# Expert numbers from bf16 step sums, lo parts kept on one engine, and a one-hot from fourfold copies: one change to a fused two-block kernel

## The chip, the cores and the metric

The kernel runs on one core of a Trainium2 chip. The metric is the device time of one execution in microseconds, as the median of several runs. The engines are named as in the profile: PE (TensorE, matmuls), PEld (its weight loads), DVE (VectorE), ACT (ScalarE), POOL (GpSimd) and SP (SyncE, which issues the DMAs).

## The reference, cut to what matters

Two blocks are applied to x of 256 tokens by 1024 features, in float32. The first is a retention and sparse-attention mixer with a gated convolution FFN. The second is a mixer of a gated linear recurrence (HGRN) and a long convolution (Hyena), and then PEER, a layer of 128 x 128 = 16384 experts. The change is in the second block, mostly in PEER:

```python
qh = (xb @ w_q).reshape(T, 8, 2, 128)
s = einsum('thpc,hpnc->thpn', qh, sk)              # scores against 2 x 128 sub-keys
s1, i1 = top_k(s[:, :, 0], 16)
s2, i2 = top_k(s[:, :, 1], 16)
cand_s = (s1[..., :, None] + s2[..., None, :]).reshape(T, 8, 256)
cand_i = (i1[..., :, None] * 128 + i2[..., None, :]).reshape(T, 8, 256)
top_s, pos = top_k(cand_s, 16)
experts = take_along_axis(cand_i, pos, axis=-1)
g = softmax(top_s)
act = gelu(einsum('td,thkd->thk', xb, u[experts])) * g
out = einsum('thk,thkd->td', act, v[experts])
```

## The kernel before, in words

**Products of float32 by two parts.** A weight tile of 128 x 1024 floats comes in by one DMA (`chunk`, tile `wraw`, four buffers). ACT writes its high part `whi` (three buffers) and then DVE or POOL writes the rest, `wlo = wraw - whi` (three buffers). A product takes three matmuls: whi with the high and the low part of the activations, then wlo with the high part. `lin_a` issues, for one chunk, 16 matmuls that read whi and then 8 that read wlo. `chunk` has an argument `pool_lo`, the share of its calls whose wlo goes to POOL.

**PEER as a dense layer.** The kernel does not gather experts. For each of the 128 values of i1 there is a chunk of u (`u_blocks`: one chunk, 24 matmuls into one PSUM tile `ax`, then ACT's gelu into the tile `gs`), and later a chunk of v (`v_blocks`). The activations are multiplied in between by a matrix of gate weights, which `weigh` makes for 8 tokens at a time: `prep` compares the key numbers with a row of numbers (the one-hot `o1` for the first key, `o2` for the second, and three bf16 parts of g in `gT` times o2), 24 small matmuls turn them into 4 x 128 x 128 weights in two `ax` tiles, and DVE (for blocks that are done) or ACT (for those that are not) puts them into `gs`. The first 48 u blocks come before `weigh` starts, the other 80 run beside it. A u block whose tokens are partly weighed keeps its gelu in a tile `gl`, and DVE multiplies it into `gs`.

**The top 16.** Sixteen chunks of w_q give the key scores; DVE finds 16 of 128 for each half (`first_tops`). The generator `topk` does the rest, 128 tokens (one half) at a time: 50 candidate sums in `cs`, the 16 best with their places `px`, then the expert numbers. For these the kernel before builds the same 50 candidates of the numbers (`ce`), compares each place with 0 to 49 (`eq`, 3200 elements for four heads), multiplies by `ce` (`em`), and adds up over the candidates (`ei`). The result is split into two key numbers by shifts of integers (`ii`, `fi`).

**The order.** The code pushes generators aside (`beside`) and takes steps from them between chunks (`pump`). In the kernel before, `pump` holds a step back while a count of DVE's work stands ahead of a count of PE's; the class `Counted` wraps both engines to keep those counts. The framework's scheduler then fixes each engine's order; every engine runs its own list in order and waits on semaphores. Through the wrapper, almost all instructions of PE and DVE carry line L220.

The four PSUM tiles `ax` are shared by u blocks, weights and transposes; the output accumulates in the other four.

Of the kernel before, what the change touches and what calls it, by code (L numbers as in the profile page):

```python
# [189 lines left out]
def tile_block(ctx: ExitStack, tc: tile.TileContext, a, out):  # L190
# [17 lines left out]

    clock = {"pe": 0.0, "dve": 0.0}

    class Counted:
        def __init__(self, engine, cost):
            self.engine, self.cost = engine, cost

        def __getattr__(self, name):
            f = getattr(self.engine, name)

            def call(*args, **kw):
                self.cost(name, args)
                return f(*args, **kw)  # L220

            return call

    def elements(ap):
        return math.prod(ap.shape[1:])

    def tensor_cost(name, args):
        n = elements(args[2])
        if name == "transpose":
            c = 0.11  # L230
        elif args[1].dtype == F32:
            c = 4 * n / 2400 + 0.005
        else:
            c = n / 2400 + (0.0135 if args[1].dtype == F32R else 0.0025)
        clock["pe"] += c

    def vector_cost(name, args):
        n = elements(args[1]) if name in ("tensor_reduce", "max") else \
            elements(args[2]) if name == "max_index" else elements(args[0])
        if args[0].dtype == BF:  # L240
            n //= 2
        clock["dve"] = max(clock["dve"], clock["pe"] - 3.0) + (n + 150) / 960

    PE, DVE = Counted(nc.tensor, tensor_cost), Counted(nc.vector, vector_cost)

    ident = cons.tile([128, 128], F32, name="ident")
    mhalf = cons.tile([128, 8], F32, name="mhalf")
    DVE.memset(mhalf, -0.5)
# [6 lines left out]
    def step():  # L255
        side = sides[0]
        try:
            next(side[0])
            side[1] = clock["dve"]
        except StopIteration:  # L260
            sides.pop(0)

    def pump(n, wait=True):


        while n > 0 and sides and (not wait or sides[0][1] <= clock["pe"]):
            step()
            n -= 1

    def beside(gen):  # L270
        sides.append([gen, 0.0])
        return gen

# [19 lines left out]
    def chunk(src, n=1024, pool_lo=0.0, gate=None):  # L293

        r = wp.tile([128, n], F32, name="wraw", bufs=NRAW)
        nc.sync.dma_start(r, src)
        hi = wp.tile([128, n], F32R, name="whi", bufs=NHI)
        if gate is not None:
            DVE.tensor_copy(hi[:, 0:1], gate[0][:, 0:1])
        nc.scalar.activation(hi, r, AF.Copy)  # L300
        lo = wp.tile([128, n], F32R, name="wlo", bufs=3)
        if gate is not None:
            DVE.tensor_copy(lo[:, 0:1], gate[1][:, 0:1])
        cnt[0] += 1
        eng = nc.gpsimd if (cnt[0] * pool_lo) % 1.0 + pool_lo >= 1.0 else DVE
        eng.tensor_tensor(lo, r, f32(hi), OP.subtract)  # L306
        return hi, lo

    def split(hi, lo, src):
        nc.scalar.activation(hi, src, AF.Copy)  # L310
        DVE.tensor_tensor(lo, src, f32(hi), OP.subtract)

    def lin_a(ps, w, xs, pool=None):

        (wh, wl), (xh, xl) = w, xs
        for k in range(8):
            s = slice(k * 128, k * 128 + 128)
            PE.matmul(ps, wh[:, s], xh[:, k, :], start=(k == 0), stop=False)
            PE.matmul(ps, wh[:, s], xl[:, k, :], start=False, stop=False)
        for k in range(8):  # L320
            s = slice(k * 128, k * 128 + 128)
            PE.matmul(ps, wl[:, s], xh[:, k, :], start=False, stop=(k == 7))

    def lin_b(ps2, w, xs, k0, nk, first, last, n=512, tiles=(0, 1)):

        (wh, wl), (xh, xl) = w, xs
        for i in tiles:
            ti = slice(i * 128, i * 128 + 128)
            for q, (wt, xt) in enumerate(((wh, xh), (wh, xl), (wl, xh))):
                for k in range(nk):  # L330
                    PE.matmul(ps2[i], xt[:, k0 + k, ti], wt[:, k * n:(k + 1) * n],
# [9 lines left out]
    def rstd_of(ss, n, scale, eps):  # L341
        DVE.tensor_scalar(ss, ss, scale, eps, op0=OP.mult, op1=OP.add)
# [6 lines left out]
    def rstd_sum(ss):  # L349
        DVE.tensor_tensor(ss[:, 0:1], ss[:, 0:1], ss[:, 1:2], OP.add)  # L350
# [8 lines left out]
    class Norm:  # L359
# [13 lines left out]
        def weigh(self, i):  # L373
            self.xw[i] = act.tile([128, D], F32, name="xn", bufs=2)
            for h in range(2):
                DVE.tensor_tensor(self.xw[i][:, half(h)], self.x[:, i, half(h)], self.nw[:, half(h)], OP.mult)

        def ready(self, i):
            r = rstd_sum(self.ss[i])
            self.dg[i] = act.tile([128, 128], F32, name="diag", bufs=2)  # L380
            DVE.tensor_scalar(self.dg[i], ident, r, None, op0=OP.mult)

        def turn(self, i):
            ti = slice(i * 128, i * 128 + 128)
# [8 lines left out]
    class Post:  # L393
# [6 lines left out]
        def piece(self, i, h, ps):  # L400
# [4 lines left out]
            DVE.tensor_tensor(self.y[i][:, half(h)], ps, self.nw[:, half(h)], OP.mult)  # L405

        def finish(self, i):
            r = rstd_sum(self.ss[i])
            for h in range(2):
                xh = self.x[:, i, half(h)]  # L410
                DVE.scalar_tensor_tensor(xh, self.y[i][:, half(h)], r, xh, op0=OP.mult, op1=OP.add)
# [10 lines left out]
    def filters(fp):  # L422
# [15 lines left out]
        for l, wt in enumerate((fw1, fw2)):  # L438
            p = pax([128, T])
            PE.matmul(p[:64], wt, hid, start=True, stop=True)  # L440
            y = fp.tile([64, T], F32, name="siny")
            DVE.tensor_scalar(y, p[:64], fvec[:, 2 * l:2 * l + 1], fvec[:, 2 * l + 1:2 * l + 2],
                                    op0=OP.add, op1=OP.mult)
            n = fp.tile([64, T], F32, name="sinn", bufs=1)
            DVE.tensor_scalar(n, y, float(np.float32(1 / (2 * math.pi))), 12582912.0, op0=OP.mult, op1=OP.add)
            DVE.tensor_scalar(n, n, -12582912.0, None, op0=OP.add)
# [10 lines left out]
        for j in range(8):  # L457
# [41 lines left out]
    for _ in range(16):  # L499
        PE.matmul(wps, warm[:, :128], warm, start=True, stop=True)  # L500
# [81 lines left out]
    def tables():  # L582
# [7 lines left out]
        DVE.tensor_copy(identb, ident)  # L590
        DVE.tensor_copy(cmask, nsac[:, 0:128])
# [14 lines left out]
    def rope_rest(dst, q, n, cos, sin):  # L606
        p2 = pax([128, T])
        PE.matmul(p2[:, :n], perm, q[:, :n], start=True, stop=True)
# [3 lines left out]
        DVE.tensor_tensor(t2[:, :n], p2[:, :n], sin, OP.mult)  # L612
        DVE.tensor_tensor(dst, t1[:, :n], t2[:, :n], OP.add)

    def proj_v():
        pv = [[pmm([128, 512]) for _ in range(2)] for _ in range(2)]
        for k in range(8):
            wh, wl = pre[k] if k < 2 else chunk(a["wb1"][k], 792)
            for i in range(2):
                ti = slice(i * 128, i * 128 + 128)  # L620
                for q, (wt, xt) in enumerate(((wh, hT[0]), (wh, hT[1]), (wl, hT[0]))):
                    st, en = (k == 0 and q == 0), (k == 7 and q == 2)
                    PE.matmul(pv[i][0], xt[:, k, ti], wt[:, 0:512], start=st, stop=en)
                    PE.matmul(pv[i][1][:, :280], xt[:, k, ti], wt[:, 512:792], start=st, stop=en)
            if k > 2:
                pump(1)
        for i in range(2):
            nc.scalar.activation(gate[:, i, :], pv[i][1][:, 256:280], AF.Sigmoid)
            DVE.tensor_copy(vb[:, i, 0:512], pv[i][0])
            DVE.tensor_copy(vb[:, i, 512:768], pv[i][1][:, 0:256])  # L630

    def proj(j, bank=pmm):
# [6 lines left out]
        elif j < 12:  # L639
            fl, pos = flat["kv"[j - 10]]  # L640
            v = ps.rearrange("p (n a b) -> p a n b", a=8, b=2)
            for g in range(2):
                gs_ = slice(g * 64, g * 64 + 64)
                for par in range(2):
                    for half in range(2):
                        hs = slice(half * 8, half * 8 + 8)
                        DVE.tensor_tensor(
                            fl[par * 64:par * 64 + 64, hs, g, 0:15], v[gs_, :, half:half + 15, par],
                            pos[gs_, par, hs].unsqueeze(2).to_broadcast([64, 8, 15]), OP.add)
        else:  # L650
            h = j - 12
            nc.scalar.activation(decay[:, h, :], ps, AF.Copy)
            DVE.tensor_scalar(silT[:, h, :], ps, gnw[:, h:h + 1], None, op0=OP.mult)

    def compress():

        hidT, w2 = {}, {}
        for s in "kv":
            fl, pos = flat[s]
            ph = pax([128, 256])  # L660
            for c in range(4):
                w1 = wp.tile([128, 4, 256], F32, name="wraw", bufs=NRAW)
# [10 lines left out]
            for c in range(2):  # L673
                PE.matmul(pt[:, c, :], part[:, c * 128:c * 128 + 128], stack, start=True, stop=True)
# [907 lines left out]
```

## Time and profile before

| | us |
|---|---|
| median of 3 runs | 1624.26 (1622.09 to 1625.32) |
| the profiled execution's own time | 1621.0 |
| its span, first to last instruction | 1619.2 |
| PE busy in the span | 1561.6 (96%) |
| DVE busy | 1166.7 (72%) |
| ACT busy | 799.8 (49%) |
| POOL busy | 368.3 (23%) |

The stages by time from the span's start: first block to 391; second block's mixer from there to 757; w_q chunks to about 816; 128 u blocks to 1263, of which the first 48 end at 985; v blocks to the end. PE's matmuls overlap, so the spacing of starts is read, not the length of one.

### The profile page before, as it was taken

Reading aid. Unit: us, or ns where it says so; the run is one execution under the profiler, and the core shown is the slowest. Engines: PE = TensorE matmul, PEld = TensorE weight load, DVE = VectorE, ACT = ScalarE, POOL = GpSimd, SP = SyncE. Lnnn points to the kernel's source line nnn. Section 1 sums busy time; section 2 is a strip of 40 time slices with the busy share of each in tenths; the row PEclk is TensorE's granted clock in tenths of the full one; section 3 lists DMA queues with packets and bytes.
Section 4 is the critical chain, followed back from the end, with each engine's and each line's share of the span. In section 5 each row is a group of like instructions: output and inputs, shape, how many; then the busy total and the mean of one; then the engine's idle time right before and its main releaser. Section 6 shows DMA issues by size and latency. Waiting matters only on the chain.

```text
span 1619.2 us, 30408 instructions
## 1 busy us (share of the span) xinstructions
PE 1561.6 (96%) x12014; PEld 1401.1 (87%) x12014; DVE 1166.7 (72%) x2041; ACT 799.8 (49%) x1383; POOL 368.3 (23%) x204
## 2 busy tenths in 40 slices
PE   8999999999999989999987899999999999999998
PEld 7775899978987977987987899999999888888886
DVE  6585787846688696775799915999999655555554
ACT  4454565545744634544543344544434455555444
POOL 0122333112112112102767861111123000000000
PEclk9999999999999999999989999999999999999999
DMA  7731555554653443554433455444444655555553
GB/s 255 253 103 37 178 181 182 193 174 159 203 183 119 158 141 108 166 179 169 160 124 119 150 190 183 146 155 147 155 144 142 210 195 193 194 190 192 194 193 117
DMA packets 78646, 268.59 MB, mean 166 GB/s; under 512 B 9991, under 2 KB 12328, under 8 KB 78376
## 3 DMA queue, kind: packets, MB, share of 16 engines
q1 hardware_dynamic: 78216, 266.13, 49.6%
q8 instruction: 94, 1.54, 0.4%
q10 hardware_dynamic: 288, 0.52, 0.1%
q14 instruction: 48, 0.39, 0.1%
HBM read 263.47 MB, written 3.15 MB: 165 GB/s over the span
## 4 chain that ended last, share of the span: by engine, by line
PE 66%; DVE 8%; issue 1%; ACT 0%; POOL 0%; POOLq 0%; DVEq 0%; ACTq 0%
PE mm L220 39%; PE ax L220 27%; DVE ei L220 1%; DVE em L220 1%; DVE eq L220 1%; DVE cs L220 1%; DVE o L220 0%; DVE ii L220 0%; DVE px L220 0%; DVE sx L220 0%; DVE hk L220 0%; DVE wlo L220 0%; DVE QA L220 0%; DVE xf L220 0%; DVE ce L220 0%
## 5 line engine op out<-in xcount | busy, mean ns | idle before, releaser
L300 ACT ACTIVATE whi<-wraw 128x1024 fp32r<-128x1024 f32 (+1 forms) x474 | 500.2, 1056 | 514.8 <-PE mm L220 340.0
L220 DVE TENSOR_TENSOR wlo<-wraw,whi 128x1024 fp32r<-128x1024 f32 (+1 forms) x365 | 444.8, 1220 | 322.1 <-ACT whi L300 316.8
L306 POOL TENSOR_TENSOR wlo<-wraw,whi 128x1024 fp32r<-128x1024 f32 x109 | 294.0, 2707 | 593.1 <-ACT whi L300 500.9
L220 PE MATMUL ax<-hThi,whi 128*128 128x256 f32 x1184 | 299.8, 290 | 12.5 <-ACT whi L300 11.7
L220 PE MATMUL ax<-hTlo,whi 128*128 128x256 f32 x1184 | 295.0, 286 | 0.2 <-DVE hTlo L220 0.2
L220 PE MATMUL mm<-whi,aa 128*128 128x512 f32 x1024 | 254.0, 389 | 0.0
L220 PEld LDWEIGHTS ax<-hThi,whi 128*128 128x128 f32 x1184 | 230.5, 195 | 13.6 <-ACT whi L300 12.1
L220 PEld LDWEIGHTS ax<-hTlo,whi 128*128 128x128 f32 x1184 | 230.9, 195 | 0.4 <-DVE hTlo L220 0.4
L220 PEld LDWEIGHTS mm<-whi,aa 128*128 128x128 f32 x1024 | 192.1, 188 | 40.1 <-ACT aa L310 0.3
L220 PE MATMUL mm<-hThi,whi 128*128 128x256 f32 x832 | 207.3, 287 | 1.5 <-ACT whi L300 1.5
L220 PE MATMUL mm<-hTlo,whi 128*128 128x256 f32 x832 | 205.2, 284 | 1.0 <-DVE hTlo L220 1.0
L220 PE MATMUL ax<-hThi,wlo 128*128 128x256 f32 x1184 | 167.8, 285 | 5.1 <-POOL wlo L306 5.1
L220 PEld LDWEIGHTS mm<-hThi,whi 128*128 128x128 f32 x832 | 159.9, 193 | 3.1 <-ACT whi L300 1.9
L220 PEld LDWEIGHTS mm<-hTlo,whi 128*128 128x128 f32 x832 | 160.3, 193 | 1.6 <-DVE hTlo L220 1.5
L220 PEld LDWEIGHTS ax<-hThi,wlo 128*128 128x128 f32 x1184 | 154.0, 193 | 6.2 <-POOL wlo L306 6.2
L220 PE MATMUL mm<-wlo,aa 128*128 128x512 f32 x512 | 137.8, 389 | 0.0
L220 PE MATMUL mm<-hThi,wlo 128*128 128x256 f32 x832 | 117.0, 283 | 0.0
L220 PEld LDWEIGHTS mm<-wlo,aa 128*128 128x128 f32 x512 | 96.1, 188 | 19.9
L220 PEld LDWEIGHTS mm<-hThi,wlo 128*128 128x128 f32 x832 | 107.4, 192 | 0.0
L220 DVE TENSOR_TENSOR o<-o,gTt 128x1024 bf16<-128x1024 bf16 x96 | 92.5, 977 | 1.1
L344 POOL TENSOR_TENSOR rstd<-ssf,mhalf 128x1 f32<-128x1 f32 x2 | 1.1, 544 | 363.1 <-DVE ssf L220 363.1
L1500 ACT ACTIVATE gs<-ax 128x300 f32<-128x300 f32 (+31 forms) x64 | 18.8, 296 | 104.4 <-DVE gs L220 93.6
(347 smaller groups left out, 2128.9 us busy)
## 6 DMA issues: line engine op xcount, KB each, us to landing
wraw<-in_pu_dram SPq DMA_DIRECT2D x128, 512.0 KB, 3.3
wraw<-in_pv_dram SPq DMA_DIRECT2D x128, 512.0 KB, 3.3
wraw<-in_wa_dram SPq DMA_DIRECT2D x64, 512.0 KB, 3.5
wraw<-in_wup_dram SPq DMA_DIRECT2D x44, 512.0 KB, 3.4
wraw<-in_wb_dram SPq DMA_DIRECT2D x32, 512.0 KB, 3.3
wraw<-in_wdn_dram SPq DMA_DIRECT2D x22, 512.0 KB, 3.3
wraw<-in_wq_dram SPq DMA_DIRECT2D x16, 512.0 KB, 3.3
wraw<-in_wo_dram SPq DMA_DIRECT2D x8, 512.0 KB, 3.3
```

What stands on the lines that cost most here:

```text
L220: return f(*args, **kw)
L300: nc.scalar.activation(hi, r, AF.Copy)
L306: eng.tensor_tensor(lo, r, f32(hi), OP.subtract)
L344: nc.gpsimd.tensor_tensor(r, ss, mhalf[:, :n], OP.pow)
L1500: nc.scalar.activation(g, pv[:, o + lo_:o + hi_], AF.Copy)
```

## The change

- `pump` takes its steps without the counts; `Counted` is gone, so PE's and DVE's instructions now carry their own lines. `topk` gets one step a block instead of two.
- `pool_lo` is left out for the mixer's chunks (0.3 before), and for the u blocks (1.0 up to block 39, 0.25 from there). Those wlo are all made by DVE. The FFN's 0.4 and w_q's 1.0 stay.
- The expert numbers come by another sum: a place is compared with the 16 first places of the candidates' rows, and the row's key number is the sum of the differences of successive keys over all rows that start at or before the place; the column's likewise after the row's start is taken off. All in bf16, as 16 x 16 x 8 elements, added by halving.
- `i1T` holds each number four times, so that o1's compare reads four equal neighbours.
- `gl` has one buffer instead of two, in the FFN and in the u blocks.

```diff
-    def pump(n, wait=True):
-        while n > 0 and sides and (not wait or sides[0][1] <= clock["pe"]):
-            step()
-            n -= 1
+    def pump(n):
+        while n > 0 and sides:
+            try:
+                next(sides[0])
+                n -= 1
+            except StopIteration:
+                sides.pop(0)
...
-            w = chunk(a["wa2"][b], pool_lo=0.3 if b >= 4 else 0.0, gate=nrm.dg if b == 0 else None)
+            w = chunk(a["wa2"][b], gate=nrm.dg if b == 0 else None)
...
-    iotac = tp.tile([128, NCD, 16], BF, name="iotac")
-    nc.gpsimd.iota(iotac, pattern=[[1, NCD], [0, 16]], base=0, channel_multiplier=0,
-                   allow_small_or_imprecise_dtypes=True)
+    rows = tp.tile([128, 3, 16, 8], BF, name="rows")
+    sizes = [nb for _, na, nb in CAND for _ in range(na)]
+    for r in range(16):
+        nc.gpsimd.memset(rows[:, 0, r], float(sum(sizes[:r])))
+        nc.gpsimd.memset(rows[:, 1, r], float(sizes[r - 1] if r else 0))
+        nc.gpsimd.memset(rows[:, 2, r], float(r))
...
+        steps = [128, 16, 16, 8]
+        def total(dst, mark, w):
+            m = tp.tile(steps, BF, name="sums", bufs=2)
+            nc.vector.tensor_tensor(m, mark, w.unsqueeze(2).to_broadcast(steps), OP.mult)
+            n = 8
+            while n > 1:
+                m2 = tp.tile([128, n, 16, 8], BF, name=f"sums{n}")
+                mm = m.rearrange("p (n two) k h -> p n two k h", two=2)
+                nc.vector.tensor_tensor(m2, mm[:, :, 0], mm[:, :, 1], OP.add)
+                m, n = m2, n // 2
+            nc.vector.tensor_tensor(dst, m[:, 0], m[:, 1], OP.add)
...
-                DVE.tensor_tensor(eq, iotac.unsqueeze(1).to_broadcast(shape),
-                                        pb[:, hs].unsqueeze(2).to_broadcast(shape), OP.is_equal)
-                DVE.tensor_tensor(em, eq, ce[:, hs].unsqueeze(3).to_broadcast(shape), OP.mult)
-                yield
-                DVE.tensor_reduce(ei[:, hs], em.rearrange("p h c k -> p h k c"), AX.X, OP.add)
...
+            nc.vector.tensor_tensor(mark, pb.unsqueeze(1).to_broadcast(steps),
+                                    rows[:, 0].unsqueeze(2).to_broadcast(steps), OP.is_ge)
+            yield
+            start = tp.tile([128, 16, 8], BF, name="start")
+            total(start, mark, rows[:, 1])
+            nc.vector.tensor_tensor(pb, pb, start, OP.subtract)
+            yield
+            total(fi[:, 0], mark, dx[:, 0])
+            yield
+            mark = tp.tile(steps, BF, name="mark", bufs=2)
+            nc.vector.tensor_tensor(mark, pb.unsqueeze(1).to_broadcast(steps),
+                                    rows[:, 2].unsqueeze(2).to_broadcast(steps), OP.is_ge)
...
+            total(fi[:, 1], mark, dx[:, 1])
...
+            nc.scalar.activation(i1T[:, ti], pt[:, 0, :].unsqueeze(2).to_broadcast([128, 128, 4]), AF.Copy)
...
-            w = chunk(a["pu"][i1], pool_lo=1.0 if i1 < 40 else 0.25)
+            w = chunk(a["pu"][i1])
...
-                gl = oh[0].tile([128, T], F32, name="gl", bufs=2)
+                gl = oh[0].tile([128, T], F32, name="gl", bufs=1)
...
-            flat = [128, 2, 4, 128]
-            o1 = oh[0].tile(flat, BF, name="o1", bufs=2)
-            DVE.tensor_tensor(o1, iota1.unsqueeze(1).unsqueeze(1).to_broadcast(flat),
-                                    i1T[:, t0:t0 + 8].rearrange("p (h t) -> p h t", h=2).unsqueeze(3).to_broadcast(flat),
-                                    OP.is_equal)
+            fours = [128, 8, 32, 4]
+            o1 = oh[0].tile([128, 2, 4, 128], BF, name="o1", bufs=2)
+            nc.vector.tensor_tensor(o1.rearrange("p h t (n f) -> p (h t) n f", f=4),
+                                    iota1.rearrange("p (n f) -> p n f", f=4).unsqueeze(1).to_broadcast(fours),
+                                    i1T[:, t0:t0 + 8].unsqueeze(2).to_broadcast(fours), OP.is_equal)
...
-    u_blocks(0, NG0, lambda k: 2)
+    u_blocks(0, NG0, lambda k: 1)
```

Three places in the built order show what moves. The first is DVE's list in the second half of `topk`, beside the early u blocks. Before, the pieces of one half stand behind each other:

```order
L220 CAST pb<-px 128x128
L220 TENSOR_TENSOR eq<-iotac,pb 128x3200
L220 TENSOR_REDUCE smx<-sx 128x8
L220 TENSOR_TENSOR em<-eq,ce 128x3200
L220 RECIPROCAL smx<-smx 128x8
L220 TENSOR_REDUCE ei<-em 128x64
L220 TENSOR_TENSOR eq<-iotac,pb 128x3200
L220 TENSOR_TENSOR sx<-sx,smx 128x128
L220 TENSOR_TENSOR em<-eq,ce 128x3200
L220 TENSOR_REDUCE ei<-em 128x64
```

Now the same place reads so (`mark` is a compare, `sums` its products and their halvings):

```order
L1377 TENSOR_TENSOR mark<-pb,rows 128x2048
L261 TENSOR_TENSOR wlo<-wraw,whi 128x1024
L1334 TENSOR_TENSOR sums<-mark,rows 128x2048
L1334 TENSOR_TENSOR sums<-mark,dx 128x2048
L1339 TENSOR_TENSOR sums_10126<-sums 128x1024
L261 TENSOR_TENSOR wlo<-wraw,whi 128x1024
L1339 TENSOR_TENSOR sums_10128<-sums_10126 128x512
L261 TENSOR_TENSOR wlo<-wraw,whi 128x1024
L1339 TENSOR_TENSOR sums_10130<-sums_10128 128x256
L1339 TENSOR_TENSOR sums_10168<-sums 128x1024
L1341 TENSOR_TENSOR start<-sums_10130 128x128
L1339 TENSOR_TENSOR sums_10170<-sums_10168 128x512
```

The u blocks' wlo, which were on POOL, now stand between the pieces in DVE's list. From the tops of the last w_q chunk to the last `fi` there are 19 of them.

The second place is POOL's list ahead of the norm of PEER, where `rstd` is the power that the norm waits for, and the two wlo around belong to w_q. Before:

```order
L1328 IOTA iotac 128x800
L306 TENSOR_TENSOR wlo<-wraw,whi 128x1024
L344 TENSOR_TENSOR rstd<-ss,mhalf 128x1 x2
L1297 IOTA iota 128x512
L1299 IOTA iota_8423 128x128
```

Now (the first two rows shown are the last of 48 fills of `rows`):

```order
L1286 MEMSET rows 128x8
L1287 MEMSET rows 128x8
L1290 MEMSET xz_8486 128x2x8
L1290 MEMSET xz_8487 128x2x8
L261 TENSOR_TENSOR wlo<-wraw,whi 128x1024
L299 TENSOR_TENSOR rstd<-ss,mhalf 128x1 x2
```

Fifty fills stand where one iota stood, ahead of a wlo and of rstd.

The third is DVE's list late beside `weigh` (the numbers behind `o` and `gs` only tell tiles apart). Before, from the compares of one group of 8 tokens to the next group:

```order
L220 TENSOR_TENSOR o_14714<-iota_8423,i1T 128x1024
L220 TENSOR_TENSOR o_14716<-iota,i2T 128x1024
L220 TENSOR_TENSOR gs_10949<-gs_10949,gl 128x232
L220 TENSOR_TENSOR o_14716<-o_14716,gTt 128x1024 x2
L220 TENSOR_TENSOR wlo<-wraw,whi 128x1024
L220 TENSOR_TENSOR o_14716<-o_14716,gTt 128x1024
L220 TENSOR_TENSOR gs_10949<-gs_10949,gl 128x232
L220 TENSOR_TENSOR wlo<-wraw,whi 128x1024
L220 TENSOR_TENSOR gs_10949<-gs_10949,gl 128x232
```

Now:

```order
L1447 TENSOR_TENSOR o_14785<-iota_8423,i1T 128x1024
L1451 TENSOR_TENSOR o_14787<-iota,i2T 128x1024
L1453 TENSOR_TENSOR o_14787<-o_14787,gTt 128x1024
L1433 TENSOR_TENSOR gs_11020<-gs_11020,gl 128x232
L1453 TENSOR_TENSOR o_14787<-o_14787,gTt 128x1024
L261 TENSOR_TENSOR wlo<-wraw,whi 128x1024
L1453 TENSOR_TENSOR o_14787<-o_14787,gTt 128x1024
L1433 TENSOR_TENSOR gs_11020<-gs_11020,gl 128x232
L261 TENSOR_TENSOR wlo<-wraw,whi 128x1024 x2
L1433 TENSOR_TENSOR gs_11020<-gs_11020,gl 128x232
```

The list is the same but for a third wlo in the group, and a product with `gl` that stands one place later.

## Rows read from the trace of the kernel before

**Rows 1.** Windows of the u blocks: us, engines' busy (instructions), PEclk, DMA share, GB/s.

```profile
833.20:921.80 88.60, 67.19 (x489) 65.70 (x488) 88.39 (x169) 33.25 (x48) 65.43 (x21) 0.87 0.38 125
921.80:985.10 63.30, 63.30 (x530) 63.30 (x529) 19.39 (x16) 29.29 (x45) 39.14 (x15) 1.00 0.53 175
985.10:1222.00 236.90, 236.90 (x2306) 235.74 (x2305) 223.86 (x346) 110.29 (x253) 47.85 (x17) 1.00 0.47 152
1222.00:1235.60 13.60, 12.01 (x123) 11.56 (x121) 13.57 (x22) 4.73 (x14) 3.96 (x1) 1.00 0.50 154
```

**Rows 2.** What PE waited for, whole span: us in total, times, longest.

```profile
PE ax L220 <- ACT whi L300: 11.7, 2, 7.4
...
PE ax L220 <- POOL wlo L306: 5.1, 4, 2.0
PE ax L220 <- DVE fi L220: 4.7, 1, 4.7
...
PE mm L220 <- DVE hy L220: 2.1, 1, 2.1
PE ax L220 <- DVE hu L220: 1.9, 1, 1.9
```

**Rows 3.** One window inside the first of rows 1.

```profile
842.00:846.00 4.00, 2.87 (x14) 2.57 (x13) 4.00 (x3) 1.49 (x3) 4.00 (x2) 0.50 0.00 0
```

**Rows 4.** DVE by shape, 833.2 to 921.8: busy us, mean ns, idle before.

```profile
L220 DVE TENSOR_REDUCE ei<-em 128x64 f32<-128x3200 f32 x4 | 23.0, 5740 | 0.0
L220 DVE TENSOR_TENSOR em<-eq,ce 128x3200 f32<-128x3200 bf16 x4 | 20.3, 5087 | 0.0
...
L220 DVE TENSOR_TENSOR sx<-sx,smx 128x128 f32<-128x128 f32 x2 | 5.0, 2490 | 0.0
```

**Rows 5.** DVE's timeline: first of one half's second tops, and what follows their last.

```profile
830.95 0.31 DVE L220 MAX8 ts<-cs 128x8 f32<-128x50 f32 x2
...
837.25 0.27 DVE L220 TENSOR_TENSOR sx<-ts 128x128 f32<-128x128 f32 x1
```

**Rows 6.** DVE's timeline beside `weigh`, late: start us, us, instruction.

```profile
1207.24 1.21 DVE L220 TENSOR_TENSOR o<-iota,i1T 128x1024 bf16<-128x1024 bf16 x1
1208.37 0.68 DVE L220 TENSOR_TENSOR o<-iota,i2T 128x1024 bf16<-128x1024 bf16 x1
1208.97 1.21 DVE L220 TENSOR_TENSOR wlo<-wraw,whi 128x1024 fp32r<-128x1024 f32 x1
1210.11 0.36 DVE L220 TENSOR_TENSOR gs<-gs,gl 128x200 f32<-128x200 f32 x1
1210.39 2.01 DVE L220 TENSOR_TENSOR o<-o,gTt 128x1024 bf16<-128x1024 bf16 x3
...
1228.34 4.09 DVE L220 TENSOR_TENSOR o<-o,gTt 128x1024 bf16<-128x1024 bf16 x3
```

**Rows 7.** POOL's timeline at the last of those.

```profile
1227.93 3.96 POOL L306 TENSOR_TENSOR wlo<-wraw,whi 128x1024 fp32r<-128x1024 f32 x1 [9.50 <-ACT whi L300]
```

**Rows 8.** The mixer near 570: DVE's and POOL's timelines.

```profile
568.02 5.95 DVE L220 TENSOR_TENSOR hb<-hb 128x256 f32<-128x256 f32 x4
...
567.94 2.41 POOL L306 TENSOR_TENSOR wlo<-wraw,whi 128x1024 fp32r<-128x1024 f32 x1 [19.70 <-ACT whi L300]
570.30 2.59 POOL L994 TENSOR_TENSOR TT<-hk,hk 128x1024 f32<-128x1024 f32 x1
```

**Rows 9.** POOL's timeline ahead of PEER's norm.

```profile
751.98 1.05 POOL L1328 IOTA iotac<- 128x800 bf16 x1
752.99 2.35 POOL L306 TENSOR_TENSOR wlo<-wraw,whi 128x1024 fp32r<-128x1024 f32 x1
...
756.10 1.07 POOL L344 TENSOR_TENSOR rstd<-ss,mhalf 128x1 f32<-128x1 f32 x2 [0.76 <-DVE ss L220]
```

**Rows 10.** POOL's fills at the span's start.

```profile
0.27 0.10 POOL L1571 MEMSET const-float32-1.0<- 128x1 f32 x1
0.31 0.10 POOL L1571 MEMSET const-bfloat16-1.0<- 128x1 bf16 x1
```

More of the change, by code (lines that the diff above doesn't have):

```diff
@@ L206, in pax @@
         return psum.tile(shape, dt, name="ax", bufs=4)
[L209 to L244, printed above, removed]
     ident = cons.tile([128, 128], F32, name="ident")
     mhalf = cons.tile([128, 8], F32, name="mhalf")
-    DVE.memset(mhalf, -0.5)
+    nc.vector.memset(mhalf, -0.5)
     def f32(ap):
@@ L253, in tile_block @@
     sides = []
[L255 to L261, printed above, removed]
-    def pump(n, wait=True):
-        while n > 0 and sides and (not wait or sides[0][1] <= clock["pe"]):
-            step()
-            n -= 1
+    def pump(n):
[5 more added lines that the diff above has]
+                sides.pop(0)
     def beside(gen):
-        sides.append([gen, 0.0])
+        sides.append(gen)
         return gen
     def finish(gen):
-        while any(side[0] is gen for side in sides):
-            step()
+        while gen in sides:
+            pump(1)
     def flush():
-        while sides:
-            step()
+        pump(1 << 30)
     def zipped(*gens):
@@ L341, in rstd_of @@
     def rstd_of(ss, n, scale, eps):
-        DVE.tensor_scalar(ss, ss, scale, eps, op0=OP.mult, op1=OP.add)
+        nc.vector.tensor_scalar(ss, ss, scale, eps, op0=OP.mult, op1=OP.add)
         r = cons.tile([128, n], F32, name="rstd", bufs=4)
@@ L349, in rstd_sum @@
     def rstd_sum(ss):
-        DVE.tensor_tensor(ss[:, 0:1], ss[:, 0:1], ss[:, 1:2], OP.add)
+        nc.vector.tensor_tensor(ss[:, 0:1], ss[:, 0:1], ss[:, 1:2], OP.add)
         return rstd_of(ss[:, 0:1], 1, 1.0 / D, 1e-6)
@@ L404, in piece @@
             square_sum(self.ss[i], h, ps)
-            DVE.tensor_tensor(self.y[i][:, half(h)], ps, self.nw[:, half(h)], OP.mult)
+            nc.vector.tensor_tensor(self.y[i][:, half(h)], ps, self.nw[:, half(h)], OP.mult)
         def finish(self, i):
@@ L410, in finish @@
                 xh = self.x[:, i, half(h)]
-                DVE.scalar_tensor_tensor(xh, self.y[i][:, half(h)], r, xh, op0=OP.mult, op1=OP.add)
+                nc.vector.scalar_tensor_tensor(xh, self.y[i][:, half(h)], r, xh, op0=OP.mult, op1=OP.add)
                 self.norm.square(i, h)
@@ L817, in scores @@
         for b in range(4):
-            (nc.gpsimd if b % 2 else DVE).tensor_tensor(
+            (nc.gpsimd if b % 2 else nc.vector).tensor_tensor(
                 PT[:, b, :, :n], PT[:, b, :, :n],
@@ L842, in values @@
                 else:
[L843 removed]
+                    nc.vector.tensor_copy(tt, p)
                 cur = (j, s, tt)
@@ L1116, in hgrn_values @@
             for c in range(4):
-                w = chunk(a["wb2"][which * 2 + gq, c], pool_lo=0.3)
+                w = chunk(a["wb2"][which * 2 + gq, c])
                 lin_b(pp, w, hT, c * 2, 2, c == 0, c == 3)
@@ L1278, in tile_block @@
             for i in range(2):
-                DVE.tensor_tensor(x[:, i, hs], x[:, i, hs], pp[i], OP.add)
+                nc.vector.tensor_tensor(x[:, i, hs], x[:, i, hs], pp[i], OP.add)
                 nrm.square(i, hf)
@@ L1420, in topk @@
+            nc.vector.tensor_tensor(pb, pb, start, OP.subtract)
+            yield
+            total(fi[:, 0], mark, dx[:, 0])
+            yield
+            mark = tp.tile(steps, BF, name="mark", bufs=2)
+            nc.vector.tensor_tensor(mark, pb.unsqueeze(1).to_broadcast(steps),
+                                    rows[:, 2].unsqueeze(2).to_broadcast(steps), OP.is_ge)
             nc.scalar.activation(sx, sx, AF.Exp)
+            yield
+            total(fi[:, 1], mark, dx[:, 1])
+            yield
@@ L1461, in u_blocks @@
             done["blocks"] = i1 + 1
-            pump(per(i1 - b0), wait)
+            pump(per(i1 - b0))
     def weigh():
```

366 lines of the change are left out of this document (177 added, 189 removed).

## The prediction

> **What bounds the kernel now.** I read the busy shares first: PE works in 96% of the span, so time can only be had where PE stands still or runs at half clock. Windows over the u blocks find that place. From 921.8 to 985.1 us PE is never idle and issues 530 matmuls in 63.3 us, 0.1194 us each, 2.87 us for the 24 of a block. The 88.6 us before, from 833.2, hold only 489; at that pace they are 58.4 us of work, so 30.2 us are lost [rows 1]. While the weights are made, from 985.1 to 1222.0, PE is busy throughout; behind that it misses 1.6 us of 13.6 [rows 1].
>
> What PE waits for is read in the list of waits: the whi of ACT (11.7 us), the wlo of POOL (5.1) and `fi` of DVE (4.7), together 21.5, all on the tile `ax`, and two waits of the mixer on `hy` and `hu`, 2.1 and 1.9 [rows 2]. The other 8.7 us of the 30.2 are the clock: 0.87 on average in that window [rows 1], and after a wait 14 matmuls take 2.87 us busy of a 4 us stretch at 0.50, that is 1.2 GHz [rows 3].
>
> The engine named is not yet the cause. DVE is busy for 88.39 of those 88.6 us [rows 1]. By shape, the products `em` and the sums `ei` alone take 20.3 and 23.0 us [rows 4]. `topk` is finished only then, its `fi` is awaited, and whi and wlo wait because their buffers come free only as PE moves. So this is a stretch bound by DVE's `topk`, beside a kernel bound by PE.
>
> **The change part by part.** *Expert numbers.* The whole loss of 30.2 us is at stake. What stands on DVE instead, for one half of the tokens: candidate sums about 0.9; the second tops 6.3, from the first of them to the next step [rows 5]; five bf16 operations of 2048 elements (two compares, three products); three sums by halving; some 1.2 of small ones. No such operation is in the trace; the nearest row is the compare `o2`, bf16 with 1024 elements, 0.60 from its start to the next, against 1.13 for the compare `o1`, whose second operand repeats one number along the row [rows 6]. The operands of the new sums run over eight contiguous numbers, as `o2` runs over four, so I take 0.60 per 1024: 5 x 1.2 = 6.0, and 0.6 + 0.35 + 0.25 + 0.2 = 1.4 for each set of halvings, 4.2. A half is 18.6, two are 37.2, and the first tops of the last w_q chunk add an estimated 2.3: 39.5. The 19 wlo that were POOL's and now stand between these steps cost 1.14 each, start to start [rows 6]: 21.7. DVE then has 61.2 us of work against PE's 19 x 2.87 = 54.5. The overhang of 6.7 is near what the three wlo buffers hold ahead, two blocks and the 16 matmuls that read whi, less the making of one: 5.7 + 1.9 - 1.1 = 6.5. PE is therefore to wait 0 to 2 us; I take 1: **-29.2**. The other end: at 1.13 per 1024 each half grows by 5 x 1.06 + 3 x 0.9 = 8, the overhang by 16, and the gain is 14. A DVE operation that lies beside POOL can also be held up: `sx` with 128 elements took 2.49 us [rows 4] and 0.27 elsewhere [rows 5]. Without POOL's wlo this cause is gone, which is why I don't take the far end.
>
> *The wlo beside `weigh`.* 80 u blocks gave POOL a quarter; the rows count 17 of them, 47.85 us [rows 1]. On DVE that is 17 x 1.14 = 19.4 more; `o1` over four equal neighbours should go from 1.13 to 0.60, 27 x 0.53 = 14.3 less. DVE's busy time was 223.86 of 236.9 [rows 1], so at worst 229: still under PE. Part of it is waiting: the same three products of a group take 2.01 us alone and 4.09 when a POOL wlo runs beside them [rows 6], and that wlo itself 3.96 [rows 7]. 17 such hold-ups of 2.1 are some 36 us, so I expect DVE near 193. What PE still missed, 1.6 us at the end of the stretch beside that very wlo, goes: **-1.5**. The bounds are -1.6 and, if occupancy were work and DVE fell behind late, +10.
> The Trainium skill (Perfetto Trace Analysis, section Identifying the Most-Contended Engine) says that for Vector the occupancy percentage is a fair measure of how close the engine is to its limit; by it DVE would be the next bound here, the +10. The trace disagrees: one operation of one shape has twice the occupancy beside POOL.
>
> *The mixer.* 18 wlo of 2.4 us leave POOL for DVE. One pair of waits is plainly of their making: at 568 us four multiplications `hb` took 5.95 us, beside a POOL wlo of 2.41 and then the product `TT` of 2.59 [rows 8]. `hy` and `hu` come late, PE waits 4.0, and an estimated 2.3 of half clock follow. The wlo goes and `TT` stays, so half is regained, -3. Against it stand 18 x 1.14 us more on DVE among the steps of the trees, hidden by PE's chunks except where a tree step is awaited: +1. Together **-2**, between -6 (all of that wait) and +4 (a few tree steps each one wlo late).
>
> *POOL's fills.* One iota of 1.05 us gives way to 50 fills, ahead of a wlo of 2.35 and of `rstd`, which had waited 0.76 for its input [rows 9], so that much is slack. PE's product with `diag` stands behind `rstd`; nothing else covers it. Fills at the span's start read 0.10 each and start 0.04 apart [rows 10]: 2 to 5 us less the iota's 1.05 and the slack. **+1.5**, between 0 and 3.3.
>
> *At nothing:* one `gl` buffer (a `gl` product takes 0.28 us, start to start [rows 6], and there are four `ax` tiles to run ahead; without them it is rival B); ACT's fourfold copies of i1T, two of about 0.6 us, under an ACT that is busy half the time; steps without counts, as the order of the mixer and FFN around PE's chunks is hardly changed.
>
> **The sum:** -29.2 - 1.5 - 2 + 1.5 = -31.2. From the profiled execution's 1621.0 that is 1589.8. The median stands 3.3 above that execution, so the median after should be about 1593.
>
> **The rivals.**
> *A, DVE stays the bound of the early u blocks.* The new sums run at the rate of the old `o1`, or wlo behind DVE's long steps starve PE. For it: 61.2 against 54.5 leaves no room. Against: the width-four `o2` row. The gain shrinks by 12 to 19: 1605 to 1612.
> *B, slower: one `gl` buffer.* A block's gelu must wait until DVE has multiplied the block before into `gs`, and that product stands behind the compares and products of the next group (1.13 + 0.60 + 2.01 = 3.7 us before [rows 6]). PE notices if gelu falls behind by more than the `ax` tiles hold, of which the weights take two. One microsecond in each of 32 groups is 32; from 31.2 / 32 = 0.98 per group on, the kernel ends at 1624 or above. Against it: DVE has room between groups once POOL's hold-ups are gone.
> *C, more from the mixer.* Other waits there turn out to be of the same kind, and the fills cost nothing: 7 to 11 more, 1582 to 1586.
> *D, occupancy is work.* DVE bounds the last blocks of `weigh`: +2 to +5, 1595 to 1598. The Trainium skill's rule on occupancy, named above, is this case.
> *E, fourfold copies don't help.* `o1` stays at 1.13. In the late groups DVE's work, about 8.4 us, meets PE's 8.3 (2.5 blocks of 2.87 and the 24 small matmuls): +3 to +7, 1596 to 1600.
>
> **How the numbers follow.** Forecast 0.67, A 0.11, B 0.05, C 0.08, D 0.05, E 0.04. The likeliest gives 1593. By its own bounds it lies between 1587 and 1599; D and E end inside or at the edge, half of C and half of A are taken in with 1584 to 1608, and what is left out is about 0.15. A difference under 0.2%, 3.2 us, can't be told from none. Only B reaches that far; with a part of it, 0.02 for no difference and 0.03 for slower; faster 0.95.
>
> **What would show it.** Right: u blocks 6 to 26 spaced 2.87 us at granted clock 1.0, no long waits of `ax` on whi, wlo or `fi`; `mark` and the products of 2048 near 1.2 us, start to start; `o1` at 0.6; the products with `gTt` near 2.0 for three everywhere; DVE's busy share beside `weigh` lower in spite of its extra wlo; the wait for `diag` up to 3 us longer; those for `hy` and `hu` halved. Wrong: PE waiting on DVE's wlo in the early blocks (A), or on gelu's `gs` and `ax` beside `weigh`, with ACT in turn waiting for a `gl` product (B).

## The result, and the profile after

The changed kernel takes 1580.8 us (median of four runs, 1580.4 to 1583.37) against 1623.76 of the kernel before (1622.09 to 1625.32). The ratio is 0.974, 95% interval 0.972 to 0.976: faster by 43 us. Forecast were 1593 us and a range of 1584 to 1608, so the direction was right, the gain is well over a third larger than predicted, and the time lies below the range. The profiled execution of after took 1580.68 us, 0.1 below its median; that of before had stood 2.8 to 3.3 below its own. Of the 12.2 us between 1593 and 1580.8, 9.1 are therefore in the terms of the sum, and 3.1 in having carried over that distance.

PE issues the same chunks in the same order in both kernels, so the starts of the same chunk's first matmul in the two traces can be subtracted. Where that difference changes, time was won or lost:

| stretch (times of before) | forecast, us | measured, us |
|---|---|---|
| first block, 0 to 394 | 0 | -0.8 |
| mixer, 394 to 641 | -2 | -7.2 |
| out projection and norm, 641 to 762 | +1.5 | -0.1 |
| w_q chunks, 762 to 830 | 0 | 0.0 |
| early u blocks, 830 to 982 | -29.2 | -30.0 |
| u blocks beside `weigh`, 982 to 1260 | -1.5 | -2.4 |
| v blocks, to the end | 0 | +0.3 |

In the windows of the kernel after (columns as in [rows 1]) the early u blocks and those beside `weigh` show it:

```profile
824.90:884.00 59.10, 59.02 (x492) 58.82 (x492) 56.04 (x159) 32.95 (x48) 0.00 (x0) 1.00 0.58 192
884.00:947.10 63.10, 63.10 (x529) 63.10 (x528) 34.06 (x44) 30.29 (x46) 0.00 (x0) 1.00 0.55 182
...
946.50:1183.90 237.40, 237.40 (x2309) 236.24 (x2308) 201.42 (x372) 115.37 (x256) 0.00 (x0) 1.00 0.48 156
1183.90:1195.30 11.40, 11.40 (x121) 11.31 (x120) 11.33 (x20) 5.42 (x14) 0.00 (x0) 1.00 0.38 106
```

Where 489 matmuls had taken 88.6 us at a mean clock of 0.87, 492 now take 59.1 at 1.00, and PE is idle for 0.08. Beside `weigh` DVE is busy for 201 us instead of 224 although it makes 69 wlo instead of 51. The list of PE's waits over the span has lost the two long waits of [rows 2] on whi and those on `fi`, on POOL's wlo and on `hy`. The one on `hu` (PE's line L1106) is still there with 1.8 us, now under the name of `TT`, whose steps stand around those of `hu` in DVE's list. Among the waits that are left are these:

```profile
PE ax L344 <- DVE diag L336: 9.4, 5, 3.6
...
PE ax L1106 <- DVE TT L1010: 1.8, 1, 1.8
...
PE ax L958 <- DVE hk L1005: 0.9, 4, 0.3
```

DVE's timeline in the early u blocks (start, us, instruction) shows the new sums and the wlo between them:

```profile
829.44 1.22 DVE L1377 TENSOR_TENSOR mark<-pb,rows 128x2048 bf16<-128x2048 bf16 x1
830.57 0.28 DVE L1395 TENSOR_REDUCE smx<-sx 128x8 f32<-128x128 f32 x1
...
833.04 1.22 DVE L1334 TENSOR_TENSOR sums<-mark,dx 128x2048 bf16<-128x2048 bf16 x1
834.17 0.68 DVE L1339 TENSOR_TENSOR sums<-sums 128x1024 bf16<-128x1024 bf16 x1
834.77 1.22 DVE L261 TENSOR_TENSOR wlo<-wraw,whi 128x1024 fp32r<-128x1024 f32 x1
835.91 0.41 DVE L1339 TENSOR_TENSOR sums<-sums 128x512 bf16<-128x512 bf16 x1
```

A compare or product of 2048 costs 1.13 from start to start, a halving to 1024 0.60, one to 512 0.34: what the width-four row of [rows 6] gave. Beside `weigh`, by shape (busy us, mean ns):

```profile
L261 DVE TENSOR_TENSOR wlo<-wraw,whi 128x1024 fp32r<-128x1024 f32 x69 | 84.3, 1222 | 35.4 <-ACT whi L255 35.1
L1453 DVE TENSOR_TENSOR o<-o,gTt 128x1024 bf16<-128x1024 bf16 x79 | 52.5, 688 | 0.9
...
L1447 DVE TENSOR_TENSOR o<-iota,i1T 128x1024 bf16<-128x1024 bf16 x27 | 18.5, 685 | 0.0
```

`o1` went from 1216 to 685 ns, the products with `gTt` from 935 on average to 688. Their row before, over the same stretch:

```profile
L220 DVE TENSOR_TENSOR o<-o,gTt 128x1024 bf16<-128x1024 bf16 x78 | 72.0, 935 | 1.0
```

### The profile page after: what moved, and what is told of

Read it like the earlier page. It is cut to its first block, busy times and chain, and to the rows that moved or that the text cites. A ratio compares the mean times of both kernels' runs of the same rounds, so it can differ in the third digit from the quotient of the medians.

```text
span 1578.9 us, 30444 instructions
## 1 busy us (share of the span) xinstructions
PE 1546.4 (98%) x12014; PEld 1388.8 (88%) x12014; DVE 1124.7 (71%) x2119; ACT 806.6 (51%) x1385; POOL 152.4 (10%) x175
## 4 chain that ended last, share of the span: by engine, by line
PE 70%; DVE 3%; issue 1%; POOL 0%; ACT 0%; POOLq 0%; ACTq 0%
PE mm L1488 22%; PE mm L286 9%; PE ax L273 8%; PE ax L277 8%; PE ax L274 8%; PE ax L1464 3%; PE mm L274 3%; PE mm L277 3%; PE mm L273 3%; PE ax L958 1%; DVE wlo L261 1%; PE ax L1116 0%; PE ax L1151 0%; PE ax L1308 0%; DVE hk L1005 0%
## 5 line engine op out<-in xcount | busy, mean ns | idle before, releaser
L261 DVE TENSOR_TENSOR wlo<-wraw,whi 128x1024 fp32r<-128x1024 f32 (+1 forms) x443 | 539.7, 1219 | 341.5 <-ACT whi L255 336.6
L273 PE MATMUL ax<-hThi,whi 128*128 128x256 f32 x1184 | 294.5, 287 | 0.7 <-ACT P L763 0.7
L274 PE MATMUL ax<-hTlo,whi 128*128 128x256 f32 x1184 | 290.3, 283 | 0.2 <-DVE hTlo L266 0.2
L273 PEld LDWEIGHTS ax<-hThi,whi 128*128 128x128 f32 x1184 | 226.8, 192 | 1.1 <-ACT P L763 0.9
L274 PEld LDWEIGHTS ax<-hTlo,whi 128*128 128x128 f32 x1184 | 227.0, 192 | 0.4 <-DVE hTlo L266 0.4
L261 POOL TENSOR_TENSOR wlo<-wraw,whi 128x1024 fp32r<-128x1024 f32 x31 | 75.2, 2424 | 191.6 <-ACT whi L255 184.3
L1453 DVE TENSOR_TENSOR o<-o,gTt 128x1024 bf16<-128x1024 bf16 x96 | 64.1, 687 | 1.0
L266 DVE TENSOR_TENSOR aa<-gs,aa 128x256 fp32r<-128x256 f32 x128 | 53.4, 418 | 1.5 <-ACT aa L265 1.4
```

Source lines behind the costliest of these rows:

```text
L266: nc.vector.tensor_tensor(lo, src, f32(hi), OP.subtract)
L273: nc.tensor.matmul(ps, wh[:, s], xh[:, k, :], start=(k == 0), stop=False)
L274: nc.tensor.matmul(ps, wh[:, s], xl[:, k, :], start=False, stop=False)
L1453: nc.vector.tensor_tensor(o2[:, k], o2[:, 2], by4(gT[:, k]), OP.mult)
```

## The experiments

Theory 1: POOL's operations with two inputs stop DVE's steps beside them, and all that the mixer won is such stops; the rival: the removed counts freed its steps. Theory 3 and its rival ask which of the two edits brought the 30 us of the early u blocks. All runs go by the same chunk starts as above. In the mixer `hy`, `hu` and `hb` are tiles of the long convolution; `hk`, `TT` and `QA` are tiles of the linear recurrence, which the code computes as a tree.

**e1, the mixer's wlo back on POOL, and e2, the kernel before with them on DVE.**

```diff
-            w = chunk(a["wa2"][b], gate=nrm.dg if b == 0 else None)
+            w = chunk(a["wa2"][b], pool_lo=0.3 if b >= 4 else 0.0, gate=nrm.dg if b == 0 else None)
```

(and the same 0.3 in the mixer's three other calls; e2 takes it out of the kernel before.)

> The changed kernel with 0.3 of the mixer's wlo on POOL again, nothing else. Theory 1 (POOL's wlo stretch DVE's steps of the mixer, and every one of PE's regained 7.4 us there is such a stretch): the mixer takes 5 to 8 us longer, 1586 to 1589 us in all, with waits on hk, hy and hu back and DVE steps beside POOL's wlo at twice their length or more. Rival 1 (the mixer gained because its steps are no longer held back by the counts of work): within 1 us of the changed kernel, about 1581.

> The kernel before with the mixer's wlo all on DVE, counts and all else kept. Theory 1: 5 to 8 us faster than before, ratio 0.995 to 0.997, all of it between 470 and 640 us of the span. Rival 1: within 1 us of before, ratio 0.9995 to 1.0005.

e1: 1589.7 us (five runs, 1584.21 to 1592.49), 8 to 9 above the changed kernel where 1586 to 1589 was expected. Its profiled execution is its fastest, and there the mixer (394 to 641) is 6.6 us longer than after, within the 5 to 8 expected and nearly all of the 7.2 that the change had won: 1.4 at 471 to 530, 5.5 at 561 to 600, -0.3 behind. The out projection behind it is 1.7 shorter, by a difference that runs without the edit show too (last section). The waits on `hu` and `hy` are back (list of PE's waits, 391 to 760), and the timelines of DVE and POOL show why:

```profile
PE ax L1106 <- DVE hu L1098: 2.8, 1, 2.8
PE mm L286 <- DVE hy L1171: 2.1, 1, 2.1
```

```profile
564.94 2.62 DVE L1128 TENSOR_TENSOR hb<-hb 128x256 f32<-128x256 f32 x1
567.48 2.62 DVE L1129 TENSOR_TENSOR hb<-hb 128x256 f32<-128x256 f32 x1
570.13 0.42 DVE L1131 TENSOR_TENSOR hb<-hb 128x256 f32<-128x256 f32 x1
```

```profile
564.86 2.42 POOL L261 TENSOR_TENSOR wlo<-wraw,whi 128x1024 fp32r<-128x1024 f32 x1 [19.70 <-ACT whi L255]
567.23 2.59 POOL L949 TENSOR_TENSOR TT<-hk,hk 128x1024 f32<-128x1024 f32 x1
```

The first `hb` lasts as long as POOL's wlo beside it, the second as long as POOL's `TT`, the third, with nothing beside it, 0.42. e2: 1611.57 us, ratio 0.994 (0.992 to 0.996), 9 us faster than before by the medians, a little more than the 5 to 8 expected; in its profile, its slowest execution, the mixer is 8.3 us shorter, and -2.9 and -4.8 of that lie at the two places where the full change has -2.1 and -4.8.

**e3, the kernel before without the counts** in FFN and mixer.

```diff
-    def pump(n, wait=True):
+    def pump(n, wait=False):
```

> The kernel before without the hold-back by counts in the FFN and the mixer (the early u blocks keep it, as they ask for it by an argument), POOL's wlo kept. Theory 1: within 1.5 us of before, ratio 0.999 to 1.001. Rival 1: 5 to 8 us faster, ratio 0.995 to 0.997, in the mixer.

1621.64 us, ratio 1.001 (0.9997 to 1.0023), and its list of PE's waits in the mixer still has:

```profile
PE ax L220 <- DVE hu L220: 2.8, 1, 2.8
...
PE mm L220 <- DVE hy L220: 2.1, 1, 2.1
```

Leaving out the counts gained nothing: in this profile the mixer is even 2.8 us longer than before. Theory 1 stands for the mixer. The early u blocks keep the counts in e3, so no run shows what leaving them out there, or `topk`'s one step a block, is worth.

**e5, the u blocks' wlo back on POOL, and e6, the old sums** with all wlo on DVE.

```diff
-            w = chunk(a["pu"][i1])
+            w = chunk(a["pu"][i1], pool_lo=1.0 if i1 < 40 else 0.25)
```

```diff
+                nc.vector.tensor_tensor(eq, iotac.unsqueeze(1).to_broadcast(shape),
+                                        pb[:, hs].unsqueeze(2).to_broadcast(shape), OP.is_equal)
+                nc.vector.tensor_tensor(em, eq, ce[:, hs].unsqueeze(3).to_broadcast(shape), OP.mult)
...
+                nc.vector.tensor_reduce(ei[:, hs], em.rearrange("p h c k -> p h k c"), AX.X, OP.add)
...
-            total(start, mark, rows[:, 1])
```

> The changed kernel with the u blocks' wlo on POOL again as before (all up to block 39, then a quarter); the new sums stay. DVE then has about 39 us of topk beside 55 us of PE's work, so by load alone nothing is lost. Theory 3 (the new sums bring nearly all of the 30 us, the wlo on DVE little): early u blocks lose 0 to 5 us, the end of weigh 2 us, 1582 to 1588. Rival 3 (POOL's wlo stretch DVE and are stretched by it, to more than PE's 2.87 us a block): 10 us or more lost in the early blocks, 1592 or above.

> The changed kernel with the old eq, em, ei sums of the expert numbers; all wlo stay on DVE. Theory 3 (load: old sums at their undisturbed lengths, about 1.7 + 3.4 + 3.4 us for four heads, make 2 x 17 us against 2 x 10 of the new, DVE has about 77 us against PE's 55 with 6.5 of slack): 12 to 18 us lost, 1593 to 1599. Rival 3 (what made the old sums long was POOL beside them, and without it they are as good as hidden): under 6 us lost, below 1587.

e5: 1603.78 us, 23 above the changed kernel; of the 30 us of the early blocks only 6.8 are won. Theory 3 (the new sums alone bring nearly all of it) falls. DVE by shape between 830.5 and 905.5 us:

```profile
L1339 DVE TENSOR_TENSOR sums<-sums 128x512 bf16<-128x512 bf16 x6 | 13.1, 2177 | 0.0
L1339 DVE TENSOR_TENSOR sums<-sums 128x1024 bf16<-128x1024 bf16 x6 | 12.9, 2150 | 0.0
L1339 DVE TENSOR_TENSOR sums<-sums 128x256 bf16<-128x256 bf16 x6 | 10.2, 1705 | 0.0
...
L1341 DVE TENSOR_TENSOR start<-sums 128x128 bf16<-128x128 bf16 x2 | 4.8, 2424 | 0.0
```

A halving of 512 elements takes 2177 ns on average instead of 410: whatever its size, a step that starts beside a wlo of POOL's lasts until that has ended. Many small steps are the worst company for POOL. What PE then waits for (822 to 947 us), and one row of ACT's timeline:

```profile
PE ax L273 <- ACT whi L255: 12.6, 1, 12.6
PE ax L273 <- DVE grest L1412: 5.7, 1, 5.7
```

```profile
856.03 0.31 ACT L1389 ACTIVATE sx<-sx 128x128 f32<-128x128 f32 x1 [16.35 <-DVE sx L1367]
```

The whi is late because ACT runs its list in order and the Exp of `sx` stands ahead of it, waiting 16.35 us for DVE. That row has its like in the trace of the kernel before, 13 us long and just ahead of the 7.4 us wait of [rows 2]:

```profile
878.07 0.31 ACT L1420 ACTIVATE sx<-sx 128x128 f32<-128x128 f32 x1 [13.00 <-DVE sx L220]
```

e6: 1600.04 us, 19 above the changed kernel; of the 30 us, 9.8 are won. PE waits 13.0 us for DVE's wlo. DVE by shape, 826 to 896:

```profile
L1376 DVE TENSOR_REDUCE ei<-em 128x64 f32<-128x3200 f32 x4 | 22.7, 5679 | 0.0
...
L1374 DVE TENSOR_TENSOR em<-eq,ce 128x3200 f32<-128x3200 bf16 x4 | 14.0, 3488 | 0.0
L1372 DVE TENSOR_TENSOR eq<-iotac,pb 128x3200 bf16<-128x3200 bf16 x4 | 7.3, 1821 | 0.0
```

Against [rows 4], `em` is shorter by a third without POOL beside it, but `ei` is not. I had expected 3.4 us for each `ei`; the four took 9 us more, and the loss lies a little above 12 to 18. Neither edit alone gives a third of the 30 us (6.8 and 9.8); both together give 30.0.

**e7, the old one-hot `o1`.**

```diff
-            fours = [128, 8, 32, 4]
...
-                                    i1T[:, t0:t0 + 8].unsqueeze(2).to_broadcast(fours), OP.is_equal)
+            flat = [128, 2, 4, 128]
...
+                                    i1T[:, t0:t0 + 8].rearrange("p (h t) -> p h t", h=2).unsqueeze(3).to_broadcast(flat),
+                                    OP.is_equal)
```

(and `i1T` holds each number once.)

> The changed kernel with the old one-hot o1 (i1T once, 1.21 us busy). DVE beside weigh goes from 201.4 to about 215.5 us of PE's 237.4. Theory (weigh is bound by PE): within 1 us of the changed kernel, 1580 to 1582. Rival E of the prediction (late groups become DVE's): 3 to 7 us slower, 1584 to 1588.

1582.55 us (1578.9 to 1582.69), a little above the 1580 to 1582 expected. Beside `weigh` its chunk starts keep the same spacing as after (982 to 1260: 0.0); its profile lost 3.6 us in the first 102 us and won 1.6 ahead of the w_q chunks. By shape `o1` is 1217 ns again:

```profile
L1447 DVE TENSOR_TENSOR o<-iota,i1T 128x1024 bf16<-128x1024 bf16 x26 | 31.6, 1217 | 0.0
```

The faster one-hot has no part in the gain. The second `gl` buffer wasn't tried.

**e8, the fills twice.**

```diff
-    for r in range(16):
+    for r in [r for r in range(16) for _ in range(2)]:
```

> The changed kernel with POOL's 48 fills of rows issued twice (the same values), 1.65 us more ahead of the wlo and rstd before PEER. Theory 4 (the fills stood in slack: the sum of squares on DVE ends with POOL's wlo in both kernels, and rstd follows at once): no slack is left, so PE's wait for diag grows from 1.9 to about 3.5 us, 1.5 to 2 us slower than the changed kernel. Rival 4 (the sum of squares, freed of the wlo beside it, ends earlier and POOL still has room): 0 to 0.5 us.

1585.06 us (1578.03 to 1585.94), too spread to tell; the trace tells. PE's product waits 3.52 us for `diag`, 1.60 more than after, as theory 4 had it:

```profile
753.94 1.27 PE L344 MATMUL ax<-diag,xn 128*128 128x128 f32 x8 [3.52 <-DVE diag L336]
```

In the kernel after itself the fills are 0.034 us apart, 48 in 1.64 us, and POOL's timeline runs on without a gap:

```profile
743.73 0.11 POOL L1285 MEMSET rows<- 128x8 bf16 x1
...
745.48 2.38 POOL L261 TENSOR_TENSOR wlo<-wraw,whi 128x1024 fp32r<-128x1024 f32 x1
747.82 1.07 POOL L299 TENSOR_TENSOR rstd<-ss,mhalf 128x1 f32<-128x1 f32 x2
```

With 0.11 for `xz` that is 1.75 us, 0.70 more than the iota and just under the slack of 0.76 in [rows 9].

**e4 and e10, the tree's sum `TT` on DVE.** In the kernel after, DVE's timeline has this row beside POOL's `TT` (565.89, 2.67 us):

```profile
566.23 3.42 DVE L951 TENSOR_TENSOR QA<-hq,hf 128x1024 f32<-128x1024 f32 x1
```

```diff
-        nc.gpsimd.tensor_tensor(TT[0], KB[0], KB[1], OP.add)
+        nc.vector.tensor_tensor(TT[0], KB[0], KB[1], OP.add)
```

> The changed kernel with the sum TT of the tree (128 x 1024, POOL's, 2.6 us) on DVE. In the changed kernel DVE's product QA beside it takes 3.42 us where it otherwise takes 1.22, and PE then waits 1.75 us for TT's successor and hu. Theory 1 (a POOL operation with two inputs in SBUF stops DVE): this wait shrinks by 1 to 2 us and its stretch at half clock goes with it, 2 to 4 us faster than the changed kernel, about 1577 to 1579. Rival 2 (DVE has too much to do there, one more operation of 1.14 us makes it later): 0 to 2 us slower, 1581 to 1583.

> TT on DVE as in the run before, now on the same chip as the changed kernel. Theory 1: 1.5 to 3 us faster than the changed kernel in the median, and no wait for hu or TT in the mixer. Rival 2: no faster.

e4: 1579.56 us (1579.36 to 1581.62). e10: 1580.19 (1578.3 to 1584.71), beside e9's 1581.37: the medians can't tell them apart, and neither shows the 1.5 to 4 us that I had expected. The profiles can at the place: in e4 `TT` and `QA` take 1.22 each on DVE, PE has no wait there, and the stretch 561 to 600 is 2.3 us shorter than after; 600 to 641 gives 0.8 back. Window 571 to 584 of e4:

```profile
571.00:584.00 13.00, 13.00 (x137) 11.25 (x137) 12.72 (x28) 5.34 (x9) 0.00 (x0) 1.00 0.55 170
```

**e9, the changed kernel again,** on the chip of e10 and e11.

> The changed kernel itself, unaltered, on the chip of the next two runs: 1579 to 1584 us. Its spread is the measure for differences of one or two microseconds between changed kernels.

1581.37 us (1580.38 to 1582.82), as expected.

**e11, `TT` and two wlo of w_q on DVE.**

```diff
-        w = chunk(a["wq"][z], pool_lo=1.0 if z else 0.0)
+        w = chunk(a["wq"][z], pool_lo=1.0 if z > 2 else 0.0)
```

(and `TT` as in e4.)

> TT on DVE, and also the wlo of the second and third w_q chunk on DVE, which in the changed kernel are POOL's and stand around the fills ahead of rstd. Theory 1: DVE's sum of squares, 2.09 us beside POOL's wlo, takes 0.15 us, rstd no longer stands behind a wlo, and PE's wait of 1.92 us for diag shrinks by 1 to 1.9 us: 1 to 2 us below TT on DVE alone. Rival 2: the two wlo, 1.14 us each, stand ahead of the sum of squares on DVE instead, and the wait stays within 0.5 us.

1577.9 us (1575.37 to 1578.17), below every run of e9 and a median of 3.5 us less: it beats both kernels. Against e10 it is 2.3 less, a little more than expected. The sum of squares takes 0.15 us instead of 2.09 and PE's wait for `diag` is 1.4 us shorter:

```profile
746.95 1.24 PE L344 MATMUL ax<-diag,xn 128*128 128x128 f32 x9 [0.54 <-DVE diag L336]
```

In the profiles the stretch from 641 to 762 is 3.0 us shorter than in e10. The other 1.6 are the granted clock behind the wait, which also stayed up in five runs without this edit (last section), so no run shows that they are its doing.

## Why the prediction was right in direction and short in size

- **The step that failed is the mixer's, -2.** It took one pair of waits, halved it because `TT` stays, and charged +1 for more wlo among the trees' steps. Measured: -7.2, beyond the -6 that the prediction had kept as its bound. Without these 5.2 us the time would have stood at 1586, inside the range. At 561 to 600 us it is -4.8 rather than -3: the wait on `hy` goes wholly, only 1.75 us for `hu` remains (named `TT` in the list of after), and the mean granted clock behind these waits rises from 0.80 to 1.00 (first rows below, of before and after). At 471 to 530 it is -2.1 that I had not priced at all, short waits on `hk` (last row below, of before; 0.9 and 0.3 are left after). The +1 did not come. e1, e2 and e3 show that POOL's wlo is the cause and the counts are not. This is rival C, which I had thought unlikely (0.08). Its mechanism came true, more from the mixer and fills that cost nothing, and with 6.8 us of the two together it stood at the lower edge of its 7 to 11; its 1582 to 1586 still misses 1580.8. C and the lower end of the range were too close to the forecast.

```profile
575.00:592.00 17.00, 12.97 (x122) 10.41 (x121) 14.06 (x28) 5.20 (x8) 2.44 (x1) 0.80 0.37 127
571.00:584.00 13.00, 11.25 (x127) 9.44 (x125) 12.41 (x25) 5.11 (x8) 0.00 (x0) 1.00 0.51 163
PE ax L220 <- DVE hk L220: 3.4, 6, 0.9
```

- **The fills: +1.5 was mis-sized,** -0.1 for the stretch. Their spacing was in [rows 10]; I took 2 to 5 us for 50 of them where 0.034 each gives 1.7, inside the slack. e8 shows that the slack is used up.
- **The early u blocks: -29.2 held,** -30.0 measured. The per-operation prices were right, PE waited 0.08 us of the 1 that I took. One link in the reading was wrong: the whi were not late for want of buffers alone, ACT's Exp stood ahead of them waiting for `topk` (read in the lists of e5 and before, not tried by a run of its own).
- **Both edits in one term:** I priced the sums at the undisturbed rate because the wlo leave POOL. e5 and e6 show that this condition carries most of the gain.
- **Beside `weigh`: -1.5, measured -2.4.** The wait goes and PE is never idle. DVE was forecast near 193 and is 201: the hold-ups were worth about 28 us, not 36 (224 + 19.4 - 14.3 - 201.4 = 27.7). The Trainium skill (Perfetto Trace Analysis, section Identifying the Most-Contended Engine) says that for Vector the occupancy percentage is a fair measure of how close the engine is to its limit; the trace disagrees, for DVE's busy time fell by 22 us while its list grew.
- **A, B, D and E did not happen.** `mark` runs at 1.13 us a step; ACT's `gl` never kept PE waiting; DVE has 36 us of room beside `weigh`; `o1` nearly halved, and e7 shows that nothing hangs on it. E had set PE's part of a late group at 8.3 us; 27 groups in 237.4 us are 8.8.
- **First block, -0.8:** the edits of the FFN's `gl` and of `pump` reach it, but in the eleven runs the stretch from 0 to 102 us differs by up to 5 us between executions of much the same code, with waits on a DMA, on whi and on `diag`. It is not put down to the change.
- **The distance from the profile to the median** was carried over as 3.3 us and came out 0.1 after, 3.1 of the 12.2 us missed. It was one execution's place among a few, so this part is chance. What spreads the runs stays open: e1's cover 8 us with POOL's wlo in the mixer, but e8's cover 8 and e2's 7 without.

## What to carry to other kernels

Where two engines disturb each other, look up every instruction that takes a multiple of its shortest duration and see what ran beside it: the list of waits names only the last link, and moving the other engine's work gave back such stops here that no wait of mine had named. Price two edits in one term only after asking what each is worth without the other. And a cheaper operation on an engine that isn't the bound (here `o1`) may buy nothing: this one didn't.

## What the runs showed of the hardware that I had not expected

- A DVE operation with two inputs in SBUF that starts beside a POOL operation with two inputs doesn't slow down in proportion, it lasts until POOL has ended: 128, 512 and 1024 elements take 2424, 2177 and 2150 ns on average in e5 (some of the 512 and 1024 met none and took 410 and 680), 220, 410 and 680 alone (the kernel after). It goes the other way too: in the kernel before a wlo of POOL's that started (at 856.42) while an `em` was running (854.13 to 859.82) took 5.65 us instead of 2.41. The Trainium skill (SBUF — State Buffer, section Who interferes with whom) says that a Vector instruction with two SBUF inputs contends with a GpSimd instruction that reads SBUF; these rows agree.
- The reduction `ei` isn't touched: it takes 5740 ns beside POOL's wlo and 5679 without. That it has one input is not the reason by itself, for another operation with one tensor, a product with a constant, was held up as well. In the kernel before it started at 859.74 beside a wlo of POOL's (856.42 to 862.07) and took 2419 ns; in e6, where POOL is idle, it took 0.22 us. Its row in the list that [rows 4] is taken from:

```profile
L220 DVE TENSOR_SCALAR xf<-xf 128x128 f32<-128x128 f32 x1 | 2.4, 2419 | 0.0
```

- After a wait of the same length for `diag` (1.92 us) the 32 small matmuls behind it took 5.44 us in the kernel after and 3.81 in e7, where the code there is the same: the granted clock fell in one execution (0.50, the 1.2 GHz level, from 750 to 752; mean 0.68 over 748.8 to 754.1) and stayed at 1.00 in the other. Behind a wait of 1.90 to 1.96 us it is 5.44 in before, after, e2, e4, e9 and e10, and 3.81 in e1, e3, e5, e6 and e7. 1.6 us of difference between runs come from this alone, and before and after are alike in it.
